# Last layer: x turned to rows of tokens by VectorE and 128-byte DMA pieces during the gate and up blocks

## The chip, the cores and the metric

The kernel runs on one core of a Trainium2 chip. The metric is the device time of one execution in microseconds, as the median of repeated runs: 1115.44 us for the kernel before. The core has five engines that work side by side: TensorE (PE, matrix products; its weight loads are listed as PEld), VectorE (DVE), ScalarE (ACT), GpSimd (POOL) and SyncE (SP), which here only issues DMAs. Sixteen DMA engines carry out what the queues issue.

## The reference, cut to what matters

An encoder of two layers on 512 tokens of width 1024, in float32. Layer 0 has latent attention, layer 1 chunked attention with a relative bias; each layer has a SwiGLU block with a hidden width of 2816 and a norm before and after it. The change touches the end of layer 1:

```python
def swiglu(h, w_gate, w_up, w_down):
    return (jax.nn.silu(h @ w_gate) * (h @ w_up)) @ w_down
...
    for layer in range(DEPTH):
        ...
        x = x + rms_norm(y, attn_post_g[layer])
        h = rms_norm(x, ffn_pre_g[layer])
        f = swiglu(h, ffn_w_gate[layer], ffn_w_up[layer], ffn_w_down[layer])
        x = x + rms_norm(f, ffn_post_g[layer])
        ...
    return x
```

The result is `x` in rows of tokens, (512, 1024). To form it the last line needs the `x` that went into the block once more, token by token.

## The kernel before, in words

Inside the layers `x` is kept with features on the partitions: eight tiles `x[k]` of 128 features by 512 tokens. Each float32 product is made of three products of a high and a low part (`whi`/`wlo` of a weight, `th`/`tl` of the data): ScalarE casts the high part (L144), VectorE subtracts to get the low part (L145).

**Gate and up blocks.** `products` walks over nine pairs of output blocks, each pair in seven steps `j` (a Strassen-like scheme with seven products in place of eight). A step has 24 matmuls of 256 columns on tiles `be`, `al`, `ga` (L1487). The weights of a pair come as four loads of 512 KB on SP's queue (L162, `raw<-in_w_pair`). VectorE forms the combinations of weights that the scheme needs (L174, `raw<-raw,raw`), and adds up the partial results (L1495, L1499, L1503, L1504, L1507); ScalarE copies others out of PSUM (L1493, L1497, L1501). `hid.add` makes combinations of the hidden blocks (L1202 to L1205). Five `raw` tiles are in rotation, so a weight load can only be issued once VectorE and ScalarE are done with an older one.

**Down block.** `down` has seven steps too, in the order A11, A22, A12, E1, E2, E3, E6, each with 66 matmuls of 512 columns (L1237) on the tiles `al`, `de`, `ga`, `be`, `al`, `al` and `be`. In the last layer (`AfterLast`) the result comes out with tokens on the partitions, in four tiles of 128 tokens, and `post.during` is called after each group of a step.

**Turning x.** Before the gate and up blocks of either layer `x` is written to DRAM as `mid`, eight stores of 256 KB (L1121). In step E1 the last layer fetches all eight tiles again (L638), and during E2 and E3 (`TURNS`) TensorE transposes them, 128x128 at a time, four to a bank (L1413); ScalarE copies a bank out as `xt` (L1415). For token tiles 0 and 1 `xt` is stored to `out` (L1417), and at the end the normed result is added to it by an accumulating DMA of POOL's queue (`scale`). For token tiles 2 and 3 `xt` stays in SBUF, and VectorE adds it to the result (`plus_x`, L1456), which is stored from there. `out` lies in DRAM as (128, 4, 1024), and the host reorders it.

**Order.** Each engine carries out its instructions in the order that a scheduler has fixed when the program is built; it works by priorities that follow the order in which the code is written. DMAs of a queue are issued in order as well, and a DMA that waits holds up those behind it.

Of the kernel before, what the change touches and what calls it, by code (L numbers as in the profile page):

```python
# [10 lines left out]
F32 = mybir.dt.float32  # L11
# [3 lines left out]
OP = mybir.AluOpType  # L15
# [3 lines left out]
D, S, P = 1024, 512, 128  # L19
KT = D // P  # L20
# [10 lines left out]
NQT = S // P  # L31
# [37 lines left out]
def trunk(ctx: ExitStack, tc: tile.TileContext, a, out):  # L69
    nc = tc.nc  # L70
    V = nc.vector
# [14 lines left out]
    def U(dt=F32, name="u"):  # L86
        return up.tile([P, S], dt, tag="u", name=name_(name), bufs=NU)
# [4 lines left out]
    def bank(tag="mm", name="b"):  # L92
        return ps.tile([P, S], F32, tag=tag, name=name_(name), bufs={"mm": 4, "s": 2, "t": 2}[tag])
# [684 lines left out]
    x = []  # L778
# [27 lines left out]
    xs, sx = [], Sum()  # L806
# [276 lines left out]
    def ffn(i, x_src, osp, firsts, late=()):  # L1083
        hp = tc.tile_pool(name=f"ffn{i}", bufs=1, reuse_waits="tile")
        st = ExitStack()
        hp = st.enter_context(hp)

        wide[0] = hp

        def H(dt=F32, name="h"):  # L1090
            return hp.tile([P, S], dt, tag="h", name=name_(name), bufs=2 * NF - 4)

        feed.room["h"] = halves_of(lambda: H(F32R, "wh"))
        x = fetch(x_src)
        post = Post(G_APOST[i], H)
        last = out_proj(osp, KT, post, firsts, 2, late)
        sx = Split(x, G_FPRE[i], H)
        xs = sx.xs
        banks = [bank(), bank(), bank("s"), bank("s")]
        ws = []  # L1100

        def half(h):
            for c in range(4):
                if not h:
                    ws.append(feed.next(1024))
                for k in (2 * c, 2 * c + 1):
                    for j in range(4):
                        mm3(banks[j][:, HALF[h]], ws[c]((k % 2) * S + j * P, P), cut(xs[k], HALF[h]),
                            k == 0, k == KT - 1)
                        yield  # L1110

        rest = half(0)
        post.apply(x, 0, sx.each)
        post.add_half(1, last, rest, 9, 14)
        run(rest)
        sx.squares(0)
        post.apply(x, 1, sx.each)
        run(half(1))
        sx.squares(1)
        for k in range(KT):  # L1120
            nc.sync.dma_start(a["mid"][:, k], x[k])  # L1121
        tb = []
        more = blocks_of(x, G_FPRE[i], H, tb)
        next(more)
        b = [bank(), bank()]
        rest = proj(2, KT, 4, xs, b)
        some(rest, 3)
        ss = sx.sum.total()
        r = rstd(ss, D)
        eps = sp.tile([P, 4], F32, tag="eps", name=f"eps_{i}", bufs=1)  # L1130
        V.tensor_scalar(eps, ss, EPS / D, EPS * EPS, op0=OP.mult, op1=OP.add)
        some(rest, 7)
        rb = spread_sb(r)
        next(more)
        banks.extend(b)
        hid = Hidden(H)


        for f in range(N_WHOLE):
            if f < 3:  # L1140
                b = banks[2 * f:2 * f + 2]
                if f == 2:
                    run(rest)
            else:
                b = [bank(), bank()]
                run(proj(2, KT, 4, xs, b))
            t = U(name="gt")
            V.tensor_tensor(t, b[0], rb, op=OP.mult)
            nc.scalar.activation(t, t, AF.Silu)
            h = hid.room()  # L1150
            V.scalar_tensor_tensor(h, t, -1.0, b[1], op0=OP.mult, op1=OP.mult)
            hid.add(h)
            if f == 1:
                next(more)
        products(xs, tb, rb, hid)
        post = (AfterLast if i else After)(i, eps, H)
        down(hid, post)
        st.close()
        return post

    class Hidden:

# [222 lines left out]
    class AfterLast(After):  # L1385


        def __init__(self, layer, eps, make):
            super().__init__(layer, eps, make)
            self.g, self.xt, self.r = [], [[None] * 2 for _ in range(NQT)], {}  # L1390

        GROUPS = ((0,), (1,), (2,), (3, 4, 5))


        TURNS = {(Down.E2, 1): ((0, 0), (0, 1)), (Down.E2, 2): ((1, 0), (1, 1)),
                 (Down.E2, 3): ((0, 2), (0, 3)), (Down.E3, 0): ((1, 2), (1, 3))}

        def during(self, j, i):
            if j == Down.E6 and self.later:
                self.later.pop(0)()  # L1400
            if j == Down.E1 and i == 3:
                self.x = fetch(a["mid"], self.make)
            if j == Down.A11 and i == 0:
                for o in range(2):
                    t = U(name="g")
                    gl = a["g_last"]
                    nc.sync.dma_start(t, bass.AP(tensor=gl.tensor, offset=gl.offset + o * S, ap=[[0, P], [1, S]]))
                    self.g.append(t)
                V.tensor_scalar(self.g[0], self.g[0], -1.0, None, op0=OP.mult)
            for o, tt in self.TURNS.get((j, i), ()):  # L1410
                b = bank("t", "xt")
                for f in range(NQT):
                    nc.tensor.transpose(b[:, f * P:f * P + P], self.x[4 * o + f][:, tt * P:tt * P + P], ident)  # L1413
                t = self.xt[tt][o] = U(name="xt")
                nc.scalar.copy(t, b)  # L1415
                if tt < 2:
                    nc.sync.dma_start(out[:, tt, o * S:o * S + S], t)  # L1417

        def rest(self, do):
            self.later.append(do)  # L1420
# [22 lines left out]
        def scale(self, i, r):  # L1443

            self.gained(1, i)
            for o in (0, 1):
                t = self.y[o][i]
                nc.scalar.activation(t, t, AF.Copy, scale=r)
                nc.gpsimd.dma_start(out[:, i, o * S:o * S + S], t, accum_op=OP.add)

        def plus_x(self, o, i, *queues):

            t, n = self.y[o][i], S // len(queues)
            for k, queue in enumerate(queues):
                c = slice(k * n, k * n + n)
                V.scalar_tensor_tensor(t[:, c], t[:, c], self.r[i], self.xt[i][o][:, c], op0=OP.mult, op1=OP.add)  # L1456
                queue.dma_start(out[:, i, o * S:o * S + S][:, c], t[:, c])

    def products(xs, tb, rb, hid):

        K2 = KT // 2
        moving = [[cut(tb[k][0], A0) for k in range(K2)], [cut(xs[k], A0) for k in range(K2)],
# [4 lines left out]
        for p in range(pairs):  # L1467
            al, ga = [], []
            be = [bank("t" if p % 2 else "s", "be") for _ in range(2)]
            gate = [U(name="gt") for _ in range(2)]  # L1470
            up_ = [U(name="ut") for _ in range(2)]
            for j in range(7):
                w = feed.next(1024, 2)
                if p + 1 == pairs and j >= 4:
                    hid.ahead(j // 5)
                if j == 1:
                    al = [bank(name="al") for _ in range(2)]
                if j == 2:
                    ga = [bank(name="ga") for _ in range(2)]
                to = (be, al, ga, al, al, al, be)[j]  # L1480
                for e in range(2):
                    o = to[e][:, A0]
                    for k in range(K2):
                        l, r = w(e * S + k * P, P), moving[j][k]
                        first_ = j < 3 and k == 0
                        for n, (c, d) in enumerate(((0, 0), (0, 1), (1, 0))):
                            nc.tensor.matmul(o, l[c], r[d], start=first_ and n == 0, stop=k == K2 - 1 and n == 2,  # L1487
                                             skip_group_check=True)
                    t, u = gate[e], up_[e]
                    if j == 0:  # L1490
                        nc.scalar.copy(u[:, A1], o)
                    elif j == 1:
                        nc.scalar.copy(t[:, A0], o)  # L1493
                    elif j == 2:
                        V.tensor_tensor(t[:, A0], t[:, A0], o, op=OP.add)  # L1495
                    elif j == 3:
                        nc.scalar.copy(t[:, A1], o)  # L1497
                    elif j == 4:
                        V.tensor_tensor(u[:, A1], o, u[:, A1], op=OP.add)  # L1499
                    elif j == 5:  # L1500
                        nc.scalar.copy(u[:, A0], o)  # L1501
                    else:
                        V.tensor_tensor(t[:, A1], t[:, A1], o, op=OP.add)  # L1503
                        V.tensor_tensor(t, t, rb, op=OP.mult)  # L1504
                        nc.scalar.activation(t, t, AF.Silu)
                        h = hid.room()
                        V.tensor_tensor(h, t, u, op=OP.mult)  # L1507
                        hid.add(h)
# [275 lines left out]
```

## Time and profile before

| | |
|---|---|
| three runs | 1116.55, 1115.43, 1115.44 us; median 1115.44 |
| the profiled execution | span of 1112.9 us from its first to its last instruction; what lies around it in a run is the 2.5 us to the median |
| PE | 1100.7 us busy, 99% of the span; clock granted: 1.00 throughout |
| PEld | 983.8 us, 88% |
| DVE | 931.1 us, 84% |
| ACT | 685.6 us, 62% |
| POOL | 68.5 us, 6% |
| gate and up pairs of layer 1 | 815.8 to 995.8 us of the span |
| down block of layer 1 | 995.8 to 1105.4 us; E2 and E3 from 1056.8 to 1090.1 |
| rest | to 1112.9 us: norm, last additions and stores |

Busy times are sums of the durations of an engine's instructions. A matmul's own duration (0.28 us for 256 columns, 0.39 us for 512) is longer than the step from its start to the next one's (0.117 and 0.227 us), since several are under way at once: for PE the distance of starts counts. The rows of the timeline give the start, the duration, the engine, the line, the operation and the tiles, and in brackets the idle time before, with what ended it.

### The profile page before, as it was taken

How to read it: one execution, taken by the hardware profiler on the slowest of the kernel's cores; microseconds unless marked ns; L12 is line 12 of the kernel's file. 1: busy time of each engine (PE TensorE's matmuls, PEld its weight loads, DVE VectorE, ACT ScalarE, POOL GpSimd, SP SyncE). 2: the span in 40 equal slices, each digit the busy share in tenths (PEclk: the TensorE clock that was granted, in tenths of full speed). 3: DMA queues.
4: the chain of work that ended last, by engine and by line, in shares of the span. 5: the costliest groups of instructions: out<-in, count | busy, mean ns of one | idle time of the engine just before them, and what ended most of it. 6: DMA issues, size and time to landing. Idle time of an engine off the chain costs nothing.

```text
span 1112.9 us, 18983 instructions
## 1 busy us (share of the span) xinstructions
PE 1100.7 (99%) x6973; PEld 983.8 (88%) x6973; DVE 931.1 (84%) x1671; ACT 685.6 (62%) x1339; POOL 68.5 (6%) x106
## 2 busy tenths in 40 slices
PE   9999999999999999999999999999999999999997
PEld 6888889999999998888888888889999999998885
DVE  7788737999989889978868878658999899889977
ACT  6576637755555556768636777666755555566675
POOL 1200000000000002400000000000000000002402
PEclk9999999999999999999999999999999999999999
DMA  7433226423332358970556665635422322459923
GB/s 237 117 107 81 72 72 213 133 73 108 95 125 96 126 168 240 148 213 28 186 152 170 156 181 146 152 121 176 141 76 95 133 81 97 137 170 294 172 55 77
DMA packets 62990, 150.85 MB, mean 136 GB/s; under 512 B 8432, under 2 KB 10224, under 8 KB 62896
## 3 DMA queue, kind: packets, MB, share of 16 engines
q1 hardware_dynamic: 55552, 136.61, 39.0%
q0 software_dynamic: 6912, 12.59, 6.9%
q8 instruction: 55, 0.90, 0.3%
q10 hardware_dynamic: 432, 0.44, 0.1%
q14 instruction: 39, 0.32, 0.1%
HBM read 119.52 MB, written 9.63 MB: 116 GB/s over the span
## 4 chain that ended last, share of the span: by engine, by line
PE 91%; DVE 3%; DMA 2%; issue 1%; ACT 1%; POOL 0%; SPq 0%; POOLq 0%; DVEq 0%; ACTq 0%
PE al L1487 17%; PE b L361 11%; PE b L362 11%; PE b L363 11%; PE be L1487 9%; PE al L1237 8%; PE be L1237 5%; PE ga L1487 4%; PE de L1237 3%; PE ga L1237 3%; PE pt L523 2%; DMA x<-in_x 1%; DVE wlo L145 1%; PE b L1643 1%; PE b L1642 1%
## 5 line engine op out<-in xcount | busy, mean ns | idle before, releaser
L144 ACT CAST whi<-raw 128x1024 fp32r<-128x1024 f32 (+3 forms) x224 | 225.2, 1007 | 203.8 <-PE al L1487 72.2
L145 DVE TENSOR_TENSOR wlo<-raw,whi 128x1024 fp32r<-128x1024 f32 (+3 forms) x224 | 260.6, 1165 | 52.2 <-ACT whi L144 51.3
L1487 PE MATMUL al<-th,whi 128*128 128x256 f32 x432 | 122.8, 284 | 0.2 <-DVE ut L1499 0.2
L1487 PE MATMUL al<-tl,whi 128*128 128x256 f32 x432 | 120.8, 280 | 0.0
L1487 PE MATMUL al<-th,wlo 128*128 128x256 f32 x432 | 120.8, 280 | 0.0
L361 PE MATMUL b<-xh,whi 128*128 128x512 f32 (+1 forms) x298 | 114.5, 385 | 0.0
L363 PE MATMUL b<-xh,wlo 128*128 128x512 f32 (+1 forms) x298 | 110.0, 369 | 0.3 <-DVE wlo L145 0.3
L362 PE MATMUL b<-xl,whi 128*128 128x512 f32 (+1 forms) x298 | 109.9, 369 | 0.0
L174 DVE TENSOR_TENSOR raw<-raw,raw 128x1024 f32<-128x1024 f32 x72 | 86.4, 1217 | 0.6 <-DMA raw<-in_w_pair 0.4
L1487 PEld LDWEIGHTS al<-th,whi 128*128 128x128 f32 x432 | 81.2, 188 | 2.5 <-DVE ut L1499 0.5
L1487 PEld LDWEIGHTS al<-tl,whi 128*128 128x128 f32 x432 | 81.3, 188 | 0.0
L1487 PEld LDWEIGHTS al<-th,wlo 128*128 128x128 f32 x432 | 81.2, 188 | 0.1
L511 ACT ACTIVATE p<-p,mn 128x128 f32<-128x128 f32 (+1 forms) x96 | 54.0, 562 | 39.5 <-DVE mn L509 38.6
L145 DVE TENSOR_TENSOR ptl<-pt,pth 128x128 fp32r<-128x128 f32 (+1 forms) x96 | 46.6, 486 | 29.4 <-ACT pth L144 23.6
L145 DVE TENSOR_TENSOR wlo<-wd,whi 128x512 fp32r<-128x512 f32 x86 | 56.4, 684 | 14.4 <-ACT whi L144 14.2
L144 ACT CAST whi<-wd 128x512 fp32r<-128x512 f32 x86 | 50.0, 619 | 25.5 <-PE al L1237 10.6
L363 PEld LDWEIGHTS b<-xh,wlo 128*128 128x128 f32 x298 | 56.2, 189 | 10.0 <-DVE wlo L145 0.7
L361 PEld LDWEIGHTS b<-xh,whi 128*128 128x128 f32 x298 | 56.4, 189 | 6.4 <-ACT whi L144 0.4
L362 PEld LDWEIGHTS b<-xl,whi 128*128 128x128 f32 x298 | 56.5, 189 | 5.6
L144 ACT CAST pth<-pt 128x128 fp32r<-128x128 f32 (+1 forms) x96 | 40.2, 420 | 26.9 <-PE pt L523 26.1
L1237 PE MATMUL al<-whi,ph 128*128 128x512 f32 x132 | 51.7, 392 | 0.0
L1237 PE MATMUL al<-whi,pl 128*128 128x512 f32 x132 | 51.6, 391 | 0.0
(315 smaller groups left out, 3272.0 us busy)
## 6 DMA issues: line engine op xcount, KB each, us to landing
raw<-in_w_pair SPq DMA_DIRECT2D x72, 512.0 KB, 3.7
wd<-in_w_down SPq DMA_DIRECT2D x54, 256.0 KB, 5.9
raw<-in_w_o SPq DMA_DIRECT2D x16, 512.0 KB, 3.5
raw<-in_w_gu SPq DMA_DIRECT2D x16, 512.0 KB, 3.7
raw<-in_w_down SPq DMA_DIRECT2D x16, 512.0 KB, 4.4
raw<-in_w_qkb SPq DMA_DIRECT2D x16, 512.0 KB, 3.7
wd<-in_w_down POOLq DMA_DIRECT2D x22, 256.0 KB, 5.5
wd<-raw POOLq DMA_DIRECT2D x22, 256.0 KB, 4.4
```

The source lines that it names most:

```text
L144: return (nc.scalar.copy(dst_hi, src), V.tensor_tensor(dst_lo, src, dst_hi.bitcast(F32), op=OP.subtract))
L145: V.tensor_tensor(dst_lo, src, dst_hi.bitcast(F32), op=OP.subtract))
L174: V.tensor_tensor(t, x, y, op=OP.add)
L361: nc.tensor.matmul(o, l[0], r[0], start=start, stop=False)
L362: nc.tensor.matmul(o, l[0], r[1], start=False, stop=False)
L363: last_mm[0] = nc.tensor.matmul(o, l[1], r[0], start=False, stop=stop)
L511: nc.scalar.activation(p[:, :n], p[:, :n], AF.Exp, bias=mn[:, :1], scale=-1.0, accum_out=self.sums[:, qt:qt + 1])
L523: nc.tensor.transpose(t[:, kt * P:(kt + 1) * P], p[:, kt * P:(kt + 1) * P], ident)
L1237: nc.tensor.matmul(to[e], l[c], r[d], start=j < 4 and k == 0 and n == 0, stop=k == NF // 2 - 1 and n == 2, skip_group_check=True)
L1487: nc.tensor.matmul(o, l[c], r[d], start=first_ and n == 0, stop=k == K2 - 1 and n == 2, skip_group_check=True)
L1642: nc.tensor.matmul(o[:, q_], vv, pth[:, kt, q_], start=kt == 0, stop=False)
L1643: nc.tensor.matmul(o[:, q_], vv, ptl[:, kt, q_], start=False, stop=kt == NQT - 1)
```

## The change

A generator `by_tokens` is stepped through by `products` of the last layer: ahead of steps 1, 3 and 5 of each pair it does one of its three stages, for one tile `k` in each of the first eight pairs. The first stage issues a load of `mid[:, k]` (256 KB, SP). The second has VectorE transpose the 128x512 tile in blocks of 32x32. The third issues four stores (SP), one for each band of 32 partitions: the band's rows hold, for each of 16 token blocks, 32 features of one token, so that a store has 512 pieces of 128 bytes, which lie 4 KB or more apart in `out`. `out` is now (512, 1024), in rows of tokens, and holds all of `x` when the down block starts. TensorE's transposes, ScalarE's copies and the four stores of `xt` are gone; in step E1 the eight loads from `mid` give way to four of 256 KB from `out`, for token tiles 2 and 3.

```diff
-        products(xs, tb, rb, hid)
+        products(xs, tb, rb, hid, by_tokens(H) if i else None)
...
+    def rows_of(tt):
+        return out[tt * P:(tt + 1) * P]
+
+    def by_tokens(make):
+
+        for k in range(KT):
+            x = make(name="x")
+            nc.sync.dma_start(x, a["mid"][:, k])
+            yield
+            t = make(name="xt")
+            V.transpose(t, x)
+            yield
+            for q in range(4):
+                nc.sync.dma_start(
+                    bass.AP(tensor=out.tensor, offset=out.offset + k * P + 32 * q, ap=[[D, 32], [32 * D, S // 32], [1, 32]]),
+                    t[32 * q:32 * q + 32].rearrange("i (b j) -> i b j", j=32))
+            yield
...
-        TURNS = {(Down.E2, 1): ((0, 0), (0, 1)), (Down.E2, 2): ((1, 0), (1, 1)),
-                 (Down.E2, 3): ((0, 2), (0, 3)), (Down.E3, 0): ((1, 2), (1, 3))}
...
             if j == Down.E1 and i == 3:
-                self.x = fetch(a["mid"], self.make)
+                for tt in range(2):
+                    self.xt[2 + tt] = [U(name="xt") for _ in range(2)]
+                    for o, t in enumerate(self.xt[2 + tt]):
+                        nc.sync.dma_start(t, rows_of(2 + tt)[:, o * S:o * S + S])
...
-            for o, tt in self.TURNS.get((j, i), ()):
-                b = bank("t", "xt")
-                for f in range(NQT):
-                    nc.tensor.transpose(b[:, f * P:f * P + P], self.x[4 * o + f][:, tt * P:tt * P + P], ident)
-                t = self.xt[tt][o] = U(name="xt")
-                nc.scalar.copy(t, b)
-                if tt < 2:
-                    nc.sync.dma_start(out[:, tt, o * S:o * S + S], t)
...
-                nc.gpsimd.dma_start(out[:, i, o * S:o * S + S], t, accum_op=OP.add)
+                nc.gpsimd.dma_start(rows_of(i)[:, o * S:o * S + S], t, accum_op=OP.add)
...
-    def products(xs, tb, rb, hid):
+    def products(xs, tb, rb, hid, aside=None):
...
             for j in range(7):
+                if aside is not None and j in (1, 3, 5):
+                    next(aside, None)
```

The lines behind the new code move by 12 or so: L1487 becomes L1499, L1495 L1507, L1497 L1509, L1499 L1511, L1503 L1515, L1504 L1516, L1507 L1519, and L1202 to L1205 become L1220 to L1223.

The scheduler puts the new instructions into the order of each engine. Three places matter. The first is VectorE in the first pair. In its rows `raw` is a weight tile or a combination, `wlo` the low part of the weight of a step, and what stands in brackets are the semaphores that the instruction waits for (DMAHW: a transfer). Before:

```order
L174 TENSOR_TENSOR raw_9547<-raw_9547,raw_9382 128x1024
L1205 SCALAR_TENSOR_TENSOR hs_9473<-hs_9471,hd_9580 128x256 [waits DVE_49]
L174 TENSOR_TENSOR raw_9626<-raw_9626,raw_9663 128x1024 [waits DMAHW2_49]
L145 TENSOR_TENSOR wlo_9632<-raw_9547,whi_9631 128x1024 [waits PE_49,Activation_49]
L145 TENSOR_TENSOR wlo_9667<-raw_9119,whi_9666 128x1024 [waits PE_49,Activation_49]
```

and now:

```order
L174 TENSOR_TENSOR raw_9547<-raw_9547,raw_9382 128x1024
L1223 SCALAR_TENSOR_TENSOR hs_9473<-hs_9471,hd_9580 128x256 [waits DVE_49]
L1171 STREAM_TRANSPOSE xt_9700<-x_9626 128x512 [waits DMAHW3_49]
L174 TENSOR_TENSOR raw_9628<-raw_9628,raw_9665 128x1024 [waits DMAHW2_49]
L145 TENSOR_TENSOR wlo_9634<-raw_9547,whi_9633 128x1024 [waits PE_49,Activation_49]
L145 TENSOR_TENSOR wlo_9669<-raw_9119,whi_9668 128x1024 [waits PE_49,Activation_49]
```

The transpose stands ahead of two weight tiles' work here, where VectorE before went on without a gap.

The second place is the middle of a later pair, the third one (even pairs look like it), first VectorE, from the additions of step 2 on. Before:

```order
L1495 TENSOR_TENSOR gt_10087<-gt_10087,ga_10165 128x256 [waits PE_49,Activation_49]
L145 TENSOR_TENSOR wlo_10195<-raw_9877,whi_10194 128x1024 [waits Activation_49]
L145 TENSOR_TENSOR wlo_10226<-raw_10010,whi_10225 128x1024 [waits PE_49,Activation_49]
L1499 TENSOR_TENSOR ut_10088<-al_10129,ut_10088 128x256 [waits PE_49]
L174 TENSOR_TENSOR raw_10504<-raw_10369,raw_10371 128x1024 [waits DMAHW5_49,DMAHW4_49,DVE_49]
```

and now:

```order
L1507 TENSOR_TENSOR gt_10103<-gt_10103,ga_10183 128x256 [waits PE_49,Activation_49]
L1171 STREAM_TRANSPOSE xt_10210<-x_10136 128x512 [waits DMAHW6_49]
L145 TENSOR_TENSOR wlo_10215<-raw_9887,whi_10214 128x1024 [waits Activation_49]
L174 TENSOR_TENSOR raw_10026<-raw_10026,raw_9959 128x1024 [waits DVE_49]
L1511 TENSOR_TENSOR ut_10104<-al_10147,ut_10104 128x256 [waits PE_49]
L145 TENSOR_TENSOR wlo_10246<-raw_10026,whi_10245 128x1024 [waits Activation_49]
L1511 TENSOR_TENSOR ut_10105<-al_10148,ut_10105 128x256 [waits PE_49]
```

The transpose follows the additions directly; the combination that needs two fresh weight loads has gone to a later place, behind the first L1516. On ScalarE at the same place (casts of weights, and copies of PSUM) the order before was

```order
L144 CAST whi_10194<-raw_9877 128x1024 [waits DMAHW5_49,PE_49]
L1497 COPY gt_10086<-al_10129 128x256 [waits PE_49]
L144 CAST whi_10225<-raw_10010 128x1024 [waits DVE_49,PE_49,Activation_49]
L1497 COPY gt_10087<-al_10130 128x256 [waits PE_49]
L144 CAST whi_10257<-raw_10255 128x1024 [waits DVE_49,PE_49]
```

and is now

```order
L144 CAST whi_10214<-raw_9887 128x1024 [waits DMAHW2_49,PE_49]
L1509 COPY gt_10102<-al_10147 128x256 [waits PE_49]
L1509 COPY gt_10103<-al_10148 128x256 [waits PE_49]
L144 CAST whi_10245<-raw_10026 128x1024 [waits DVE_49,Activation_49]
L144 CAST whi_10281<-raw_10279 128x1024 [waits PE_49,Activation_49]
```

Both copies now stand ahead of the cast; in odd pairs one stays behind it, as before.

The third place is SP's queue in the same pair. Before it held weight loads alone; now it reads

```order
L162 DMA raw_10212<-in_w_pair 128x1024 [waits DMAHW5_49,DVE_49]
L1168 DMA x_10136<-mid 128x512 [waits DMAHW6_49]
L162 DMA raw_10395<-in_w_pair 128x1024 [waits DMAHW7_49,DVE_49]
L1174 DMA out_x<-xt_10210 32x16x32 [waits DMAHW0_49,DVE_49]
L1174 DMA out_x<-xt_10210 32x16x32 [waits DMAHW1_49]
L1174 DMA out_x<-xt_10210 32x16x32 [waits DMAHW2_49]
L1174 DMA out_x<-xt_10210 32x16x32 [waits DMAHW3_49]
L162 DMA raw_10397<-in_w_pair 128x1024 [waits DMAHW4_49,DVE_49]
L162 DMA raw_10432<-in_w_pair 128x1024 [waits DMAHW5_49,DVE_49]
```

Two of the pair's four weight loads stand behind the four stores, which wait for the transpose, and the combination `raw_10536<-raw_10395,raw_10397` (L174) on VectorE waits for the first of them.

More of the change, by code (lines that the diff above doesn't have):

```diff
@@ L1389, in __init__ @@
             super().__init__(layer, eps, make)
-            self.g, self.xt, self.r = [], [[None] * 2 for _ in range(NQT)], {}
+            self.g, self.xt, self.r = [], {}, {}
         GROUPS = ((0,), (1,), (2,), (3, 4, 5))
-        TURNS = {(Down.E2, 1): ((0, 0), (0, 1)), (Down.E2, 2): ((1, 0), (1, 1)),
-                 (Down.E2, 3): ((0, 2), (0, 3)), (Down.E3, 0): ((1, 2), (1, 3))}
         def during(self, j, i):
@@ L1456, in plus_x @@
                 V.scalar_tensor_tensor(t[:, c], t[:, c], self.r[i], self.xt[i][o][:, c], op0=OP.mult, op1=OP.add)
-                queue.dma_start(out[:, i, o * S:o * S + S][:, c], t[:, c])
-    def products(xs, tb, rb, hid):
+                queue.dma_start(rows_of(i)[:, o * S:o * S + S][:, c], t[:, c])
+    def products(xs, tb, rb, hid, aside=None):
         K2 = KT // 2
@@ L1774 @@
         aps[name] = nc.dram_tensor(f"in_{name}", v.shape, mybir.dt.from_np(v.dtype), kind="ExternalInput").ap()
-    out = nc.dram_tensor("out_x", (P, NQT, D), F32, kind="ExternalOutput").ap()
+    out = nc.dram_tensor("out_x", (S, D), F32, kind="ExternalOutput").ap()
     aps["rot"] = nc.dram_tensor("rot", (3, 32, S), F32, kind="Internal").ap()
@@ L1781 @@
     r = run_bass_kernel_spmd(nc, [arrays], core_ids=[0])
-    y = np.asarray(r.results[0]["out_x"])
-    return np.ascontiguousarray(y.transpose(1, 0, 2).reshape(S, D))[None]
+    return np.ascontiguousarray(np.asarray(r.results[0]["out_x"]))[None]
```

## The prediction

> **What bounds the kernel now.** I read the page first: shares, queues, chain.
>
> ```profile
> span 1112.9 us, 18983 instructions
> ...
> PE 1100.7 (99%) x6973; PEld 983.8 (88%) x6973; DVE 931.1 (84%) x1671; ACT 685.6 (62%) x1339; POOL 68.5 (6%) x106
> ...
> q1 hardware_dynamic: 55552, 136.61, 39.0%
> q10 hardware_dynamic: 432, 0.44, 0.1%
> ...
> PE 91%; DVE 3%; DMA 2%; issue 1%; ACT 1%; POOL 0%; SPq 0%; POOLq 0%; DVEq 0%; ACTq 0%
> ```
>
> PE is busy 99% and carries 91% of the chain that ends last: time taken off PE comes off the end, if nothing else is late in its place. The span is 1112.9 us; the median of 1115.44 lies 2.5 us above it, and I add my sum to the median. Next the busy times by stretch: four gate and up pairs, the whole of that stage, then E2 and E3.
>
> ```profile
> core 0: us, PE busy (x) PEld busy (x) DVE busy (x) ACT busy (x) POOL busy (x), PEclk, DMA share, GB/s
> 815.80:835.70 19.90, 19.90 (x169) 19.82 (x168) 19.16 (x25) 11.16 (x17) 0.00 (x0) 1.00 0.33 107
> 835.70:855.60 19.90, 19.90 (x169) 19.78 (x168) 19.45 (x27) 10.91 (x17) 0.00 (x0) 1.00 0.32 106
> 875.40:895.10 19.70, 19.70 (x168) 19.58 (x167) 18.03 (x25) 10.98 (x17) 0.00 (x0) 1.00 0.31 108
> 815.80:995.80 180.00, 179.75 (x1514) 178.45 (x1513) 164.37 (x227) 99.99 (x157) 0.00 (x0) 1.00 0.36 118
> 1056.80:1090.10 33.30, 33.30 (x163) 27.82 (x162) 22.92 (x35) 24.35 (x47) 0.54 (x1) 1.00 0.18 48
> ```
>
> The work leaves a stretch where PE alone is full (last row: DVE 69%, ACT 73%, DMA engines 18%) and goes to one where VectorE is nearly full too (91% over the stage, 96 and 98% in its first two pairs) while DMA has room (0.36). So the gain can be read off PE, and the cost hangs on VectorE's and the queue's gaps.
>
> **The gain.** The groups of the two lines that go, and their pieces in the chain of waits (start, us):
>
> ```profile
> L1413 PE MATMUL xt<-ident,x x32: 270/272/273, 1044.6 to 1077.7; 128*128 128x128 f32 x32
> L1415 ACT COPY xt<-xt x8: 574/586/596, 1063.4 to 1078.4; 128x512 f32<-128x512 f32 x8
> ...
> 1062.37 0.66 PE xt L1413 x6
> 1065.80 0.87 PE xt L1413 x8
> 1069.42 0.87 PE xt L1413 x8
> 1077.14 0.87 PE xt L1413 x8
> ```
>
> A transpose's own 0.272 us overlaps its neighbours; the chain has what it takes of PE: 0.66 + 3 x 0.87 = 3.27 us for thirty. [...] Together **-3.6 us**. The eight ScalarE copies (8 x 0.59) and four stores ran beside PE in that stretch, and their removal is worth nothing. Nothing else is late there next: with 30 us of PE work left in E2 and E3, DVE has 22.9 and ACT 24.4 less 4.7. The eight loads in E1 become four of the same size: no PE instruction waits for them now, only additions after 1100, and I put that at zero.
>
> **The transposes on VectorE.** No such instruction is in the trace. Nearest by size is the 128x512 addition; next up stands one of 128x1024, next down one of 128x256:
>
> ```profile
> L1504 DVE TENSOR_TENSOR gt<-gt,bc 128x512 f32<-128x512 f32 x17 | 11.1, 684 | 0.1
> ...
> 885.20 0.74 DVE L1495 TENSOR_TENSOR gt<-gt,ga 128x256 f32<-128x256 f32 x2
> 885.91 1.22 DVE L145 TENSOR_TENSOR wlo<-raw,whi 128x1024 fp32r<-128x1024 f32 x1
> 888.81 1.23 DVE L145 TENSOR_TENSOR wlo<-raw,whi 128x1024 fp32r<-128x1024 f32 x1 [1.67 <-ACT whi L144]
> ```
>
> I bound it by 0.4 and 1.2 us and take 0.68 (0.6 from start to start), as nearest in columns. VectorE idles 1.67 us in a steady pair, waiting for a cast, just where the order puts the transpose (behind the additions of step 2). 0.6 fits into 1.67: **no cost in pairs 2 to 7**. At 1.2 us the fit is bare, and a pair could lose about 0.1.
>
> [...]
>
> Pair 0 has no gap where the transpose lands. DVE rows, then PE's, in that pair:
>
> ```profile
> 821.90 0.42 DVE L1205 SCALAR_TENSOR_TENSOR hs<-hs,hd 128x256 f32<-128x256 f32 x1
> 822.24 1.22 DVE L174 TENSOR_TENSOR raw<-raw,raw 128x1024 f32<-128x1024 f32 x1
> 823.37 2.35 DVE L145 TENSOR_TENSOR wlo<-raw,whi 128x1024 fp32r<-128x1024 f32 x2
> ...
> 824.28 0.28 PE L1487 MATMUL al<-th,whi 128*128 128x256 f32 x1
> 824.75 0.28 PE L1487 MATMUL al<-th,wlo 128*128 128x256 f32 x1
> ```
>
> The first `wlo` of 823.37 ends at 824.59 (+1.22), and PE uses it at 824.75: 0.16 us to spare. A transpose of 0.6 ahead of it makes PE wait 0.45. In pairs 0 and 1 together VectorE has 38.6 of 39.8 us of work; 1.2 more fill them, and I add 0.15 for what no longer fits. **+0.6 us**.
>
> **ScalarE's order.** Once in a pair PE's pace breaks, because a copy out of `al` stands behind a cast:
>
> ```profile
> 887.73 1.05 ACT L144 CAST whi<-raw 128x1024 fp32r<-128x1024 f32 x1 [0.98 <-PE al L1487]
> 888.68 0.37 ACT L1497 COPY gt<-al 128x256 f32<-128x256 f32 x1
> ...
> 888.91 0.28 PE L1487 MATMUL al<-th,wlo 128*128 128x256 f32 x1
> 889.10 0.39 PE L1487 MATMUL al<-th,whi 128*128 128x256 f32 x1
> 889.32 0.28 PE L1487 MATMUL al<-tl,whi 128*128 128x256 f32 x1
> ```
>
> PE's two steps here take 0.41 us, against 0.23 for two at its pace (24 matmuls x 7 steps in 19.7 us). In pairs 2, 4 and 6 both copies now stand ahead of the cast: 3 x 0.18 = **-0.5 us**.
>
> **The queue.** Eight loads and 32 stores are new on SP's queue in this stage, ahead of weight loads.
>
> ```profile
> raw<-in_w_pair SPq DMA_DIRECT2D x72, 512.0 KB, 3.7
> mid<-x SPq DMA_DIRECT2D x16, 256.0 KB, 2.3
> x<-mid SPq DMA_DIRECT2D x16, 256.0 KB, 4.8
> qr<-rh SPq DMA_DIRECT2D x16, 64.0 KB, 2.0
> rot<-sincos SPq DMA_DIRECT2D x4, 48.0 KB, 1.7
> ...
> L638 SPq DMA_DIRECT2D x<-mid x8: 319/323/327, 1014.3 to 1048.2; - x8
> ...
> 792.80 163.69 SPq L162 DMA_DIRECT2D raw<-in_w_pair  x32
> ...
> 896.99 1.29 DVE L1504 TENSOR_TENSOR gt<-gt,bc 128x512 f32<-128x512 f32 x2
> ```
>
> The queue itself is free (issuing takes 0.32 us; 32 weight loads are spread over 164 us). The loads of `x` land in 4.8 us or less and are issued half a pair or more ahead. The price of a 128-byte piece isn't in the trace. The page's queues bound it: q1 spends 39.0% x 16 x 1112.9 us / 55552 = 125 ns on a packet of 2459 bytes, q10 0.1% of the same, 17.8 us, / 432 = 41 ns on one of 1 KB; in proportion to bytes 128 would take 5 to 7 ns. Small writes of 48 KB land in 1.7 us. I take 20 ns, in the lower part, since 41 ns is already for eight times the bytes. Four stores put 4 x 512 / 16 = 128 pieces on each DMA engine: 2.6 us; at 41 ns 5.2, at 125 ns 16.
>
> What waits: in even pairs two weight loads stand behind the stores. In the steady pair's times the transpose would end at 886.6 (885.94 and 0.65), and the combination that needs the load comes behind the first L1504, at 897.6. Of these 11.0 us the load takes 3.7: the stores may take 7.3 us, that is 57 ns a piece. **No cost** at 20, nor at 41. In odd pairs the store stands behind the loads that are wanted soon.
>
> **Sum.** -3.6 + 0.6 - 0.5 + 0 = -3.5 us: a span of 1109.4 and a time of **1111.9 us**.
>
> **The rivals.**
>
> *The pieces choke the queue (slower).* In pairs 0, 2, 4 and 6 the weight load behind the stores is late, VectorE's combination with it, and PE waits for `wlo`. It begins beyond 57 ns a piece; VectorE's leftover gap (1.67 - 0.6) takes up another 1.1 us, to 66 ns. The loss outweighs 3.5 us when each of the four pairs loses 0.9 (73 ns), and shows as slower from 1.4 us each (77 ns). At 85 ns the four stores take 10.9 us, 2.5 too many: 4 x 2.5 - 3.5 = +6.5, **1122 us**. For it: 125 ns for a mean packet, and pieces far apart in DRAM. Against: q10's 41 ns, and the stage's DMA share of 0.36. 12 in 100.
>
> [...]
>
> *VectorE has no room after all (about the same).* Its instructions go in order, so a gap before one wait need not be usable: if all eight transposes add 0.6 to PE's time, the sum is -3.6 + 8 x 0.6 - 0.5 = +0.7, **1116.1 us**; a transpose of 1.7 us comes out alike: 0.5 beyond the fit in seven pairs, 1.5 in pair 0, +0.9 in all. For it: 96 and 98% in the first pairs. Against: 18.0 of 19.7 us in the later ones, and the gap stands where the transpose does. 23 in 100.
>
> *Cover without a gain.* PE's 3.6 us in E2 and E3 could have hidden a wait that now shows, ahead of the sums at the end. The chain runs through PE from 1056 to 1102 without another engine, so 2 in 100, at 1115.
>
> **How the numbers follow.** The forecast has 63 in 100 and its own range: a transpose of 0.4 us (0.25 in pair 0) and all nine breaks of ScalarE's gone (1.6) give -5.0, 1110.4; one of 1.2 (1.05 in pair 0, 0.1 in six pairs, 0.3 for pair 1, no gain from ScalarE) gives -3.6 + 2.0 = -1.6, 1113.8. A measurement of this kernel can tell some 0.2%, 2.2 us, from no change. The forecast is below 1113.2 in most of its cases: 0.62 faster; slower is the first rival beyond 77 ns and the far end of the second, 0.13; the rest, 0.25, the same. The range takes in the second rival up to its 1116.1 and leaves out the first: 1110.4 to 1116.3.
>
> **What will show it.** Right: E1 to E3 shorter by 3.6 us, pairs 2 to 8 at 19.7 us or less, a wait of PE for `wlo` of half a microsecond in pair 0 alone, VectorE's gap in a steady pair down from 1.7 to about 1, stores that land within 5 us. Wrong: stores that land in 8 us or more and combinations (L174) that wait for weight loads; or transposes of over 1.2 us, with PE waiting for `wlo` in every pair.

## The result, and the profile after

The changed kernel takes 1113.07 us (median of 13 runs, 1112.06 to 1114.42) against 1116.01 us for the kernel before in the same set (13 runs): a ratio of 0.9974, 95% interval 0.9966 to 0.9982. That is 2.9 us less, between 2.0 and 3.8; forecast were 3.5 less. The page of the changed kernel's profiled execution:

```profile
span 1111.4 us, 18953 instructions
...
PE 1098.7 (99%) x6941; PEld 980.9 (88%) x6941; DVE 936.2 (84%) x1679; ACT 682.5 (61%) x1331; POOL 68.3 (6%) x106
...
q1 hardware_dynamic: 72448, 138.71, 40.2%
...
PE 90%; DVE 5%; DMA 2%; issue 2%; ACT 1%; POOL 0%; DVEq 0%; POOLq 0%; SPq 0%; ACTq 0%
```

VectorE carries 5% of the chain in place of 3%. To see where time went, cut the span at marks that both programs have: the first matmul of a gate and up pair, of A11, E1 and E6. E1 to E6, before and then after (windows; columns as in the prediction's):

```profile
1041.39:1090.12 48.73, 48.73 (x231) 40.38 (x230) 37.35 (x58) 35.01 (x66) 6.42 (x8) 1.00 0.42 91
1043.30:1088.61 45.31, 45.31 (x199) 36.99 (x198) 36.96 (x58) 31.14 (x58) 6.15 (x7) 1.00 0.38 74
```

Those 3.4 us are the gain. The gate and up stage went from 179.95 to 180.49 us, A11 to E1 (45.6 and 45.5) and E6 to the end (22.8 both) stayed. The changed kernel's first pair starts 1.4 us later in its profiled execution, but every engine's order is the same up to there, so that is chance between executions (1.1 us of it are gaps between PE's matmuls in layer 0's gate and up stage), and the spans differ by 1.5 us only. The new work itself (one line's durations in ns: min, median, max; then the DMA list):

```profile
L1171 DVE STREAM_TRANSPOSE xt<-x x8: 698/704/708, 823.7 to 970.3; 128x512 f32<-128x512 f32 x8
L1174 SPq DMA_DIRECT2D out_x<-xt x32: 337/482/1614, 824.4 to 972.5; - x32
out_x<-xt SPq DMA_DIRECT2D x32, 64.0 KB, 3.0
```

A transpose takes 0.70 us, a store lands in 3.0. The pieces' price comes from the page's queue lines: q1's share of 16 engines' span rose from 6945 to 7149 us (39.0% of 16 x 1112.9, 40.2% of 16 x 1111.4) for 16896 more packets, some 12 ns apiece. The trace's own records of the 16384 pieces of 128 bytes have 13 ns on average.

For the gate and up stage I use one number throughout: PE's **breaks**. Its matmuls of 256 columns start 0.115 to 0.122 us apart where nothing holds them up; a distance above 0.135 is a break, and what it has over 0.117 is lost. The mean distance outside breaks is PE's **pace**. From the trace's start times, summed from step 2 of a pair to step 2 of the next (the last column is what follows the ninth pair's step 2):

| kernel | 0 | 1 | 2 | 3 | 4 | 5 | 6 | 7 | rest | sum, us |
|---|---|---|---|---|---|---|---|---|---|---|
| before | .11 | .18 | .71 | .18 | .20 | .20 | .20 | .20 | .19 | 2.17 |
| after | .60 | .26 | 0 | .40 | 0 | .42 | .12 | .41 | .20 | 2.41 |

So 0.24 of the stage's 0.54 us are breaks: +0.5 in pair 0, +0.2 in three odd pairs, -0.7, -0.2 and -0.1 in pairs 2, 4 and 6. The rest is pace, of which more in the last section. Pair 0, VectorE and then PE:

```profile
823.67 0.71 DVE L1171 STREAM_TRANSPOSE xt<-x 128x512 f32<-128x512 f32 x1
824.30 1.19 DVE L174 TENSOR_TENSOR raw<-raw,raw 128x1024 f32<-128x1024 f32 x1
825.41 2.35 DVE L145 TENSOR_TENSOR wlo<-raw,whi 128x1024 fp32r<-128x1024 f32 x2
...
826.07 0.28 PE L1499 MATMUL al<-tl,whi 128*128 128x256 f32 x1
826.68 0.39 PE L1499 MATMUL al<-th,wlo 128*128 128x256 f32 x1 [0.33 <-DVE wlo L145]
```

The transpose holds up the combination and the `wlo` behind it; PE stands for 0.61 - 0.12 = 0.49 us. Pair 3, VectorE and PE:

```profile
889.09 1.22 DVE L174 TENSOR_TENSOR raw<-raw,raw 128x1024 f32<-128x1024 f32 x1
890.22 0.70 DVE L1171 STREAM_TRANSPOSE xt<-x 128x512 f32<-128x512 f32 x1
890.85 1.18 DVE L145 TENSOR_TENSOR wlo<-raw,whi 128x1024 fp32r<-128x1024 f32 x1
891.95 0.74 DVE L1511 TENSOR_TENSOR ut<-al,ut 128x256 f32<-128x256 f32 x2
...
891.95 0.28 PE L1499 MATMUL be<-xl,whi 128*128 128x256 f32 x1
892.09 0.39 PE L1499 MATMUL be<-xh,wlo 128*128 128x256 f32 x1
892.31 0.28 PE L1499 MATMUL be<-xh,whi 128*128 128x256 f32 x1
892.43 0.38 PE L1499 MATMUL al<-th,whi 128*128 128x256 f32 x1
892.64 0.28 PE L1499 MATMUL al<-tl,whi 128*128 128x256 f32 x1
```

Here the gap holds not the transpose alone but a combination too: 1.13 + 0.63 = 1.76 us for a gap of 1.67. VectorE has no idle time left in the stretch, `wlo` ends at 892.03 just when PE wants it, and the addition to `ut` frees `al` late: two short breaks that the kernel before did not have there.

The long break in pair 2 of the kernel before comes from a weight load. VectorE and PE there, before:

```profile
870.22 1.23 DVE L174 TENSOR_TENSOR raw<-raw,raw 128x1024 f32<-128x1024 f32 x1 [0.44 <-DMA raw<-in_w_pair]
871.36 0.42 DVE L1499 TENSOR_TENSOR ut<-al,ut 128x256 f32<-128x256 f32 x1
...
871.83 0.38 PE L1487 MATMUL al<-th,whi 128*128 128x256 f32 x1 [0.25 <-DVE ut L1499]
```

The combination waits 0.44 us for the load, the addition behind it frees `al` late, and PE loses 0.41 us. Such breaks come and go where the program is the same: in layer 0's pairs 1 and 2, whose breaks sum to 0.19 and 0.18 us in the kernel before, they sum to 0.80 and 0.64 in the changed one, with VectorE waiting 0.55 and 0.42 for a load.

### The profile page after: what moved, and what is told of

It is laid out like the page before. It is cut to its first block, busy times and chain, and to the rows that moved or that the text cites. A ratio compares the mean times of both kernels' runs of the same rounds, so it can differ in the third digit from the quotient of the medians.

```text
span 1111.4 us, 18953 instructions
## 1 busy us (share of the span) xinstructions
PE 1098.7 (99%) x6941; PEld 980.9 (88%) x6941; DVE 936.2 (84%) x1679; ACT 682.5 (61%) x1331; POOL 68.3 (6%) x106
## 3 DMA queue, kind: packets, MB, share of 16 engines
q1 hardware_dynamic: 72448, 138.71, 40.2%
## 4 chain that ended last, share of the span: by engine, by line
PE 90%; DVE 5%; DMA 2%; issue 2%; ACT 1%; POOL 0%; DVEq 0%; POOLq 0%; SPq 0%; ACTq 0%
PE al L1499 17%; PE b L361 11%; PE b L362 11%; PE b L363 11%; PE be L1499 8%; PE al L1255 8%; PE be L1255 5%; PE ga L1499 4%; PE de L1255 3%; PE ga L1255 3%; PE pt L523 2%; DVE wlo L145 2%; DMA x<-in_x 1%; DMA raw<-in_w_pair 1%; PE b L1655 1%
## 5 line engine op out<-in xcount | busy, mean ns | idle before, releaser
L1499 PE MATMUL al<-th,whi 128*128 128x256 f32 x432 | 122.9, 285 | 0.5 <-DVE ut L1511 0.5
L1499 PE MATMUL al<-th,wlo 128*128 128x256 f32 x432 | 121.0, 281 | 0.3 <-DVE wlo L145 0.3
L1499 PE MATMUL al<-tl,whi 128*128 128x256 f32 x432 | 120.9, 280 | 0.0
L174 DVE TENSOR_TENSOR raw<-raw,raw 128x1024 f32<-128x1024 f32 x72 | 86.9, 1218 | 2.5 <-DMA raw<-in_w_pair 2.2
L1499 PEld LDWEIGHTS al<-th,whi 128*128 128x128 f32 x432 | 81.3, 188 | 2.8 <-DVE ut L1511 0.9
L1499 PEld LDWEIGHTS al<-th,wlo 128*128 128x128 f32 x432 | 81.2, 188 | 0.6 <-DVE wlo L145 0.5
L1499 PEld LDWEIGHTS al<-tl,whi 128*128 128x128 f32 x432 | 81.3, 188 | 0.0
```

The source lines that it names most:

```text
L174: V.tensor_tensor(t, x, y, op=OP.add)
```

## The experiments

Each kernel's ratio is to the kernel before, run beside it. The breaks of all of them stand in a table at the end of the section.

**The gain alone, and the cost alone.** `e_gain` is the kernel before without the transposes and ScalarE's copies of them:

```diff
             for o, tt in self.TURNS.get((j, i), ()):
-                b = bank("t", "xt")
-                for f in range(NQT):
-                    nc.tensor.transpose(...)
-                t = self.xt[tt][o] = U(name="xt")
-                nc.scalar.copy(t, b)
+                t = self.xt[tt][o] = self.x[tt * 2 + o]
```

> The kernel before without the 32 TensorE transposes and the eight ScalarE copies, and with nothing in their place: the eight loads in E1 and the four stores stay, and the tiles that are added at the end hold x as loaded (features in the place of tokens). My account: the whole gain is PE's own time in E1 to E3. From the first matmul of E1 to the first of E6 it takes 45.3 us in place of 48.7, the gate and up stage (first al of the first pair to A11) stays at 177.1, and the time falls by 3.5 us, to about 0.9969 of the kernel before. Rival (the transposes were partly a cover for a wait): E1 to E3 shorten by less than 3 us, and a wait of PE for wlo or ph shows there.

`e_stage` is the changed kernel with `TURNS`, its loads and stores back, and the new stores sent elsewhere:

```diff
-                    bass.AP(tensor=out.tensor, offset=out.offset + k * P + 32 * q, ...
+                    bass.AP(tensor=a["side"].tensor, offset=a["side"].offset + k * P + 32 * q, ...
...
+            for o, tt in self.TURNS.get((j, i), ()):    # and TURNS, as before
```

> The changed kernel with the 32 TensorE transposes, the ScalarE copies, the loads of x in E1 and the stores of xt put back; what the new stage stores goes to a DRAM tensor of its own. So it is the new stage's cost alone. My account: it costs what the traces show in the gate and up stage, 177.7 us against 177.1: time up by 0.5 us, about 1.0005, with E1 to E6 at 48.7. Rival (the stage's loads and stores disturb what follows, or VectorE has no room): stage above 179, time up by 2 us or more.

Measured: `e_gain` 0.9976 (0.9966 to 0.9987), `e_stage` 1.0005 (0.9997 to 1.0014). E1 to E6, `e_gain` first:

```profile
1043.05:1088.38 45.33, 45.33 (x199) 36.99 (x198) 36.99 (x58) 31.20 (x58) 8.66 (x10) 1.00 0.38 63
1042.38:1091.05 48.67, 48.67 (x232) 40.37 (x230) 37.35 (x58) 35.02 (x66) 6.13 (x7) 1.00 0.40 88
```

The 3.4 us go with the transposes and their copies alone and come back with them. `e_stage` has 2.36 us of breaks, as the changed kernel (2.41); its half microsecond of cost isn't told from nothing by its interval. Gain and cost lie in different stages and, within the intervals, add up. `e_gain`'s time fell by 2.7 us, not 3.5, within its interval (1.4 to 3.8).

**Where the cost lies.** `e_later` starts in pair 1 and gives the transpose a lower priority:

```diff
-                if aside is not None and j in (1, 3, 5):
+                if aside is not None and p > 0 and j in (1, 3, 5):
...
-            V.transpose(t, x)
+            with first(-60):
+                V.transpose(t, x)
```

> The changed kernel with nothing new in the first pair (tiles 0 to 7 in pairs 1 to 8), and with the transpose given a lower priority, so that in nearly all pairs it stands behind the weight subtraction of step 5, alone in VectorE's gap, and the combination L174 that stood with it in odd pairs goes back to its old place. My account of the 0.5 us that the stage lost: 0.6 in the first pair and 0.2 in each odd pair, where combination (1.13) and transpose (0.62) together are longer than the gap of 1.67; less what ScalarE's order gained in even pairs (0.9). With both losses gone, and ScalarE's order back to that of before, the stage takes 177.1 us as in the kernel before, and PE has no wait of 0.5 us for wlo: time 0.5 us under the changed kernel, 3.5 under the one before (0.9969). Rival (the pieces of 128 bytes, not the transposes' place, cost the odd pairs their time): the odd pairs stay 0.2 us longer than before, stage 177.9 or more.

Measured: 0.9977 (0.9968 to 0.9986); in time not to be told from the changed kernel. In the profile pair 0 has its 0.10 us again, odd pairs 0.19 or 0.20, pairs 2, 4 and 6 as well (0.20, 0.18, 0.18): 1.64 us of breaks, 0.5 under the kernel before, where my account had put it level; the long break of that kernel's pair 2 did not come back, which can be chance, as layer 0 shows. The stage takes 179.7 us (the expectation's 177.1 counts from a mark 2.8 us later, so 179.9). The pieces are the same as in the changed kernel, so the odd pairs' loss was VectorE's crowding. What the even pairs had gained is gone with the order.

**ScalarE's order.** `e_best` adds that order by hand, in all pairs of both layers:

```diff
                     elif j == 3:
-                        nc.scalar.copy(t[:, A1], o)
+                        feed.behind[feed.pos + 2] = (nc.scalar.copy(t[:, A1], o),)
```

> As e_later, and in every pair the cast of step 6's weight is issued behind the second copy of step 3 on ScalarE (an order fixed for the scheduler, no new work), as the scheduler happened to put it in pairs 2, 4 and 6 of the changed kernel. My account: the break of 0.18 us in PE's pace goes from eight pairs, and the one of 0.4 us in pair 2 too, where VectorE was late: stage 177.1 - 8 x 0.18 - 0.2 = 175.5 us, time 5.1 us under the kernel before (0.9954) and 2.1 under the changed one. Rival (the cast is then late in its turn, and VectorE's subtraction and PE's step 6 with it): stage 177 or more.

Measured: 1.0053 (1.0039 to 1.0066), against my 0.9954. Pair 4 there, ScalarE, VectorE and PE:

```profile
910.91 0.38 ACT L1510 COPY gt<-al 128x256 f32<-128x256 f32 x1 [1.05 <-PE al L1500]
911.18 1.05 ACT L144 CAST whi<-raw 128x1024 fp32r<-128x1024 f32 x1
...
912.26 1.22 DVE L145 TENSOR_TENSOR wlo<-raw,whi 128x1024 fp32r<-128x1024 f32 x1 [1.10 <-ACT whi L144]
913.41 0.42 DVE L1512 TENSOR_TENSOR ut<-al,ut 128x256 f32<-128x256 f32 x1
...
913.68 0.28 PE L1500 MATMUL be<-xl,whi 128*128 128x256 f32 x1
913.88 0.39 PE L1500 MATMUL al<-th,whi 128*128 128x256 f32 x1
914.10 0.28 PE L1500 MATMUL al<-tl,whi 128*128 128x256 f32 x1
```

The copies are on time and that break is gone. But the later cast delays `wlo`, the addition to `ut` stands behind it on VectorE, and PE now waits for `al` to come free: 0.19 us in the pair, as before. The breaks sum to 2.0 us. So the account of ScalarE's order was half of the cause. The loss of time lies elsewhere: A11 to E1 takes 50.3 us, 4.7 more, with PE waiting for the first down operands (waits in that stretch: total, times, longest), and layer 0 shows the same waits at its down block (2.5 us more there).

```profile
PE al L1256 <- ACT ph L144: 2.5, 2, 1.5
PE al L1256 <- DVE pl L145: 1.2, 1, 1.2
```

In the last pair the operands of the down block are prepared behind the casts; the later kernels leave the last pair out and lose nothing there (45.6 us). That it was this cast is inferred, and wasn't tried by itself.

**Both orders.** `e_sums` takes the order from the changed kernel's even pairs as a whole: the combination of step 6 goes behind VectorE's subtraction of step 5, and the cast and the subtraction of step 6 follow by themselves. `e_order` is that edit in the kernel before; `e_both` is `e_sums` with the edit in both layers.

```diff
+                if aside is not None and j == 3 and p + 1 < pairs:
+                    feed.late[feed.pos + 2] = low[0]       # the last subtraction
...
-                    src.sums(gain)
+                    with behind(self.late.get(j)):
+                        src.sums(gain)
```

> As e_later, and the combination of weights for step 6 (L174) is issued behind VectorE's subtraction of step 5 in the first eight pairs. That is the order in which the changed kernel's pairs 2, 4 and 6 ran at 19.71 us without a break: VectorE does both additions of step 2, transpose, subtraction of step 5, combination of step 6, first addition of step 4, subtraction of step 6; the cast of step 6 then comes behind both of ScalarE's copies by itself. My account after e_best: it takes both, the copies ahead of the cast and the addition of step 4 ahead of the subtraction; the copies alone only moved the break. So the two breaks (0.2 us together) go from seven or eight pairs: PE's breaks in the stage 1.6 -> 0.3 us, and the time 1.3 us under e_later, about 0.9965 of the kernel before. Rival (the breaks belong to VectorE's load, and come back elsewhere as in e_best): breaks of 1.4 us or more, time as e_later.

> The kernel before, with only this order edit (the combination of step 6 behind the subtraction of step 5, in the first eight pairs of the last layer); TensorE transposes stay. It asks whether what the changed kernel gained in pairs 2, 4 and 6 has anything to do with turning x. My account: no, it is an order that the scheduler fell into. Breaks in the stage 2.2 -> 0.4 us, time 1.8 us less, 0.9984; E1 to E6 stays at 48.7. Rival (VectorE's order only pays with the transpose in the gap): breaks stay at 2 us.

> e_sums with its order edit in the gate and up stage of both layers: the best that these experiments point to. In layer 1 PE's breaks fell from 2.2 us (kernel before) to 0.9 by it; e_order, the edit alone, had 0.2. Layer 0 runs the same code without the transposes, and its breaks should fall as in e_order, by 1.9 us. My account: -3.4 (E1 to E6) - 1.3 - 1.9 = -6.6 us, 0.9941 of the kernel before. Rival (what PE saves in breaks it loses in pace, as e_order's 0.9993 for 1.9 us may hint): 0.997, as e_sums.

Measured: `e_sums` 0.9974 (0.9965 to 0.9983), `e_order` 0.9993 (0.9984 to 1.0002), `e_both` 0.9948 (0.9935 to 0.9960). Breaks: 0.89, 0.24 and 1.74 us in layer 1 (0.9 was expected for `e_both` too); in layer 0 `e_both` has 0.28 against 1.67 before. The order removes the breaks, also without the transpose in the gap: in pairs 1 to 7 of `e_order` there is none. In `e_both`'s layer 0 VectorE still waits for weight loads in three pairs (up to 0.83 us), but no break comes of it. The times gave less than the breaks for `e_sums` (0.9965 expected, at the interval's edge) and `e_order` (0.9984, likewise). The pace of PE, which differs between executions, may be the reason; with one profile of each kernel that isn't shown. Pair 4, whole, in `e_order`, `e_sums` and `e_gain`:

```profile
901.25:920.97 19.72, 19.72 (x171) 19.72 (x169) 18.55 (x25) 11.21 (x18) 0.00 (x0) 1.00 0.33 107
900.97:921.12 20.15, 20.15 (x170) 20.00 (x169) 18.77 (x24) 12.11 (x18) 0.00 (x0) 1.00 0.55 157
902.57:922.69 20.12, 20.12 (x170) 20.00 (x169) 18.45 (x24) 10.98 (x17) 0.00 (x0) 1.00 0.32 105
```

The first has no break; the other two have 0.2 us each, and the other 0.2 are matmuls that start 0.1187 us apart on average in place of 0.1173, at a printed clock of 1.00.

What `e_sums` and `e_both` still lose in pairs 4 and 6 has PE waiting for VectorE, which has a transpose there ahead of the work that PE waits for; `e_order`, without these transposes, loses nothing in either. In `e_both`, pairs 4 and 6:

```profile
903.81 0.38 PE L1506 MATMUL al<-th,wlo 128*128 128x256 f32 x1 [0.30 <-DVE wlo L145]
...
951.03 0.39 PE L1506 MATMUL al<-th,whi 128*128 128x256 f32 x1 [0.32 <-DVE ut L1518]
```

So in these two pairs VectorE's crowding seems to be back; that is read off the order and was not tried by itself. `e_both` is the version that beats both kernels: 5.8 us under the kernel before (4.5 to 7.3), where E1 to E6, the two layers' breaks and nothing else would give 3.5 + 0.4 + 1.4 = 5.3.

**VectorE's room.** `e_twice` does each transpose twice (one more `V.transpose(t, x)`).

> The changed kernel with each VectorE transpose done twice into the same tile (0.63 us more per pair, same DMAs): it asks how much room VectorE has. My account: the gap of a steady pair is 1.67; two transposes (1.26) fit where they are alone in it, not beside a combination. Breaks of PE in the stage 2.4 us now; pair 0 +0.6, odd pairs +0.4 each, even pairs +0.1: about 5 us, time 2.6 us above the changed kernel, 1.0000 of the one before. Rival (VectorE full: each transpose adds its whole time): breaks 7.5 us, time +5 us, 1.0019. Rival (room everywhere): breaks 3.0 or less.

Measured: 0.9980 (0.9971 to 0.9989), 3.39 us of breaks. Eight more transposes, 5 us of VectorE's time, cost 1.0 us in breaks, and most of it stands in one place, pair 6 with 1.32. VectorE and PE there:

```profile
948.58 0.69 DVE L1172 STREAM_TRANSPOSE xt<-x 128x512 f32<-128x512 f32 x1
949.20 1.18 DVE L174 TENSOR_TENSOR raw<-raw,raw 128x1024 f32<-128x1024 f32 x1
...
951.55 1.23 DVE L145 TENSOR_TENSOR wlo<-raw,whi 128x1024 fp32r<-128x1024 f32 x1 [0.84 <-ACT whi L144]
952.70 0.42 DVE L1512 TENSOR_TENSOR ut<-al,ut 128x256 f32<-128x256 f32 x1
...
953.17 0.40 PE L1500 MATMUL al<-th,whi 128*128 128x256 f32 x1 [0.72 <-DVE ut L1512]
```

The second transpose holds up the combination, ScalarE's cast follows that, and the addition that frees `al` comes behind the subtraction that waits for the cast. (The wait of 1.4 us for a weight load, listed below, lies 18 us earlier, in pair 5, whose breaks are no more than in the kernel before.) My account (5 us) was too high, and the rival that VectorE is full is out. The scheduler had put the second transposes apart from the first ones. VectorE's waits in the stage, total, times and longest, before, after, and in `e_twice`:

```profile
DVE wlo L145 <- ACT whi L144: 14.1, 13, 1.7
```

```profile
DVE wlo L145 <- ACT whi L144: 7.6, 14, 1.6
```

```profile
DVE wlo L145 <- ACT whi L144: 5.2, 8, 1.6
DVE raw L174 <- DMA raw<-in_w_pair: 1.4, 1, 1.4
```

In `e_twice` 8.9 of the 10 us that the 16 transposes take are taken from the wait for casts (`wlo`), 2.4 of them by the second eight.

**The pieces.** `e_four` and `e_two` issue each store four times and twice:

```diff
-                nc.sync.dma_start(bass.AP(tensor=out.tensor, ...), t[32 * q:32 * q + 32]...)
+                for to in (out, a["side0"], a["side1"], a["side2"]):     # e_two: the first two
+                    nc.sync.dma_start(bass.AP(tensor=to.tensor, ...), t[32 * q:32 * q + 32]...)
```

> The changed kernel with each store of pieces issued four times (once to out, three times to DRAM tensors of their own): 16 stores, 8192 pieces of 128 bytes a pair. It asks from where the pieces do cost. My account: a piece takes 13 ns of a DMA engine, so 512 pieces take each engine 6.7 us; SP needs 16 x 0.5 = 8 us to issue them, some 6 us more than now, so that the weight load behind them lands 1 to 2 us after the combination wants it. VectorE has about 1 us to spare: PE loses up to 1 us a pair where a load stands behind the stores, 3 us in all (stage 183.5, time about 1.0000 of the kernel before), with DVE waits for raw<-in_w_pair of 1 us and more. Rival (pieces are far from mattering): stage as in the changed kernel. Rival (they choke the engines): over 3 us a pair, stage above 200.

> The changed kernel with each store of pieces issued twice (eight stores, 4096 pieces a pair; the second to a DRAM tensor of its own). After e_four: there a pair lost 10 us, not 1, though a store still took SP 0.5 us and landed in 2 us; the scheduler had put all four weight loads of a pair behind the 16 stores, and these wait for the transpose. My account: it is the place in the queue, not the pieces, that costs. Eight stores take SP 4.4 us, within the 7.3 us that the combination's place leaves, and here only one or two loads stand behind them: PE's breaks in the stage stay at 2 to 3.5 us, time within 1 us of the changed kernel, 0.9978. Rival (the pieces themselves choke the engines from four stores on): a third of e_four's loss, 3 us a pair, time 1.02.

Measured: `e_four` 1.0572 (1.0558 to 1.0587), `e_two` 0.9971 (0.9960 to 0.9982). With four times the stores a pair takes up to 30.2 us; with twice, the breaks sum to 2.41 us, as in the changed kernel. What is wrong in `e_four` is not the pieces' time on the DMA engines. Its waits on SP and on PE, then its line of stores and the DMA list:

```profile
SPq L1175 <- DVE xt L1171: 118.8, 8, 18.2
PE be L1500 <- ACT whi L144: 39.6, 6, 6.8
L1175 SPq DMA_DIRECT2D side<-xt x96: 303/504/1850, 822.6 to 1033.4; - x96
side<-xt SPq DMA_DIRECT2D x96, 64.0 KB, 2.0
```

A store still takes SP 0.5 us and lands in 2.0. But the scheduler put all four weight loads of a pair behind the 16 stores. SP waits 118.8 us at the head of its queue for eight transposes, then issues stores for 8.6 to 9.9 us, and only then the weights, which the next pair needs at once. From pair 2 on PE's breaks sum to 7.4 to 10.4 us a pair, about what issuing the stores takes. My account had the issue time right, and missed the order: since that changed with the dose, the run doesn't price the pieces, and a price beyond eight stores a pair stays open.

| kernel | 0 | 1 | 2 | 3 | 4 | 5 | 6 | 7 | rest | sum, us |
|---|---|---|---|---|---|---|---|---|---|---|
| e_gain | .10 | .20 | .54 | .21 | .19 | .19 | .19 | .19 | .19 | 2.00 |
| e_stage | .60 | .46 | 0 | .43 | 0 | .27 | 0 | .42 | .18 | 2.36 |
| e_later | .10 | .19 | .20 | .19 | .18 | .20 | .18 | .20 | .20 | 1.64 |
| e_best | .11 | .23 | .41 | .22 | .19 | .19 | .22 | .22 | .23 | 2.02 |
| e_sums | .04 | 0 | 0 | 0 | .22 | 0 | .45 | 0 | .18 | 0.89 |
| e_order | .05 | 0 | 0 | 0 | 0 | 0 | 0 | 0 | .19 | 0.24 |
| e_both | .03 | 0 | 0 | .17 | .57 | 0 | .59 | .17 | .21 | 1.74 |
| e_twice | .60 | .39 | 0 | .28 | .18 | .20 | 1.32 | .22 | .20 | 3.39 |
| e_two | .59 | .24 | .19 | .30 | .26 | .20 | .20 | .24 | .19 | 2.41 |

## Why the prediction was right, point by point

- **The gain, -3.6 us.** Right: -3.42 from E1 to E6, and -3.40 with the removal alone. Reading PE's share off the chain, not off the transposes' own durations (32 x 0.27 = 8.6 us), gave it. Thirty transposes in E2 and E3 were worth 3.45 us in place of 3.27, and nothing else was late there (from 1058 to 1091 the trace of the changed kernel lists no wait of PE). The other 0.3 of the 3.6 stood for the two in E1, and no run shows it: E1 took 15.37 us with them and 15.39 without. Before, they stood around a weight load of PE that waits 0.19 us for VectorE's `wlo`; in the changed kernel the weight loads there wait 0.37 us for `wlo` and 0.30 for `pl`, and the same five products take 1.51 us (from 1046.02) without the transposes and took 1.50 (from 1044.11) with them.
- **The transpose, 0.68 us and 0.6 from start to start.** Right: 0.70 and 0.63.
- **No cost in pairs 2 to 7.** Half wrong. The step that failed is the claim that the gap stands where the transpose does: true in the even pairs, but in odd ones the order of the changed kernel, open to be read, has a combination in the gap beside it. Three odd pairs lost 0.2 us each against the kernel before, and `e_later` gave it back.
- **Pair 0, +0.6.** Right: +0.49 there and +0.08 in pair 1; it goes when the first pair is left out.
- **ScalarE's order, -0.5.** Right in sign, -1.0 in size, and wrong in cause. The breaks in pairs 2, 4 and 6 went because the combination stood later, which orders ScalarE and VectorE both; the copies alone moved the break (`e_best`). 0.5 of the 1.0 is the long break of the kernel before in pair 2, which I had not counted; the rest is what was forecast. `e_gain`, with the same program in this stage, has 0.3 of that long break, and in layer 0 such breaks come and go, so how much of the 0.5 the new order took away stays open.
- **The queue, 0.** Right: a piece takes 12 or 13 ns, under the 20 that I took and twice the 6.5 that q1's mean packet of before gives in proportion to bytes (125 ns for 2459), and twice the stores cost nothing (`e_two`: breaks of 2.41 us, as in the changed kernel). The 57 ns were not put to the test. The first rival's mechanism, a weight load behind stores, is real (`e_four`), but there the load's place in the queue, behind all that SP had to issue, decided it, and not the time of a piece on a DMA engine.
- **The sum, -3.5.** The parts measure -3.4 + 0.2 in breaks, with another 0.3 of pace in the one profiled execution; the runs say -2.9, from -3.8 to -2.0. The errors in the odd pairs (some 0.6 too little) and in the even ones (0.5 too little gain) cancelled: by luck the sum was better than its terms.

## What to carry to other kernels

Work that moved off a full engine was worth its steps on that engine's chain here (3.45 us, with 3.27 read off the chain), and it cost what it met in the order of the engine that took it over (0.49 us in pair 0, 0.2 in three odd pairs): read that order in each variant of the loop body (odd and even pairs here), not in one. A short break that recurs in every turn is worth following through all engines in the loop, since putting right the one that is named last can just hand the wait to the next (`e_best`: 0.19 us in pair 4, against 0.20 before). And where a transfer waits for a computation at the head of an in-order queue, what stands behind it can matter far more than what the transfer itself takes, as in `e_four` (118.8 us of waits at the head of the queue, 2.0 us from a store's issue to its landing).

## What was not expected of the hardware

PE's pace on the same instructions has two values that differ by 1.2% (0.1173 or 0.1187 us a matmul; pair 4 above), at a mean granted clock of 0.998 or 0.999 for the whole execution in both cases. Over a stage of 180 us that is up to 2 us, as much as the effects sought here. By the start times of the twelve traces the pace holds from one break to the next: it changes in between in 6 of 233 stretches of 20 matmuls or more, and otherwise at a break or not at all. So a break can cost more than its own length, or give it back (in the changed kernel the 198 matmuls behind pair 0's break of 0.49 us start 0.1186 us apart, 0.26 us in all above 0.1173; the 320 behind the next break, of 0.08 us, go at 0.1173 again), and a stage without breaks keeps the pace it has: `e_order` ran 1317 matmuls on end at 0.1173, `e_both`'s layer 0 1375 at 0.1187. Which pace follows a break I could not tie to what a kernel does, and what sets it stays open. So a single span can't settle a microsecond in this kernel; breaks, which are counted apart from pace, can be compared, though some of them (0.3 to 0.8 us in one pair) come and go as well in layer 0, whose program most of these kernels share.
